# Shifting split weights by 128 and 448 bytes against the activations in a two-layer encoder

## The chip, the cores and the metric

The kernel runs on one core of a Trainium2 chip. The metric is the time of one execution on the device, in microseconds (us).

## The reference

A two-layer encoder over one sequence of 256 tokens of width 1024, all float32. Each layer normalises, multiplies with one wide matrix, runs four mixers side by side (gated linear attention, dilated attention, differential attention, a long convolution), weighs their projections with gates, adds the result, and runs an MLP:

```python
for i in range(DEPTH):                       # DEPTH = 2
    h = rmsnorm(x, norm1_g[i])
    z = h @ w_in[i]                          # 1024 x 11040
    ...
    ya, yb, yc, yd = mixers of the parts of z
    gt = jax.nn.sigmoid(gates.reshape(B, S, N_BRANCH, D_MODEL))
    m = (gt[:, :, 0] * (ya @ proj_a[i]) + gt[:, :, 1] * (yb @ proj_b[i])
         + gt[:, :, 2] * (yc @ proj_c[i]) + gt[:, :, 3] * (yd @ proj_d[i]))
    x = x + m @ w_out[i]
    h2 = rmsnorm(x, norm2_g[i])
    x = x + jnp.square(jax.nn.relu(h2 @ mlp_w1[i])) @ mlp_w2[i]
```

## The kernel before

All large products are done in three matmuls each, with operands split into a rounded upper part and a remainder: upper times upper, upper times lower, lower times upper (`mm3`, L237 to L241, one line for each of the three). The split of activations is kept in tiles `act` (or `h`, `lo`, `u`); the split of weights is made on the way: `load_raw` brings a unit of weights from HBM into one of three slots of the pool `wp` (L206), and `split_to` (L210) makes of each half of it an upper part `hi` on ScalarE (L221) and a lower part `lo` on VectorE (L222), in the pool `hp`, five slots each, some halves ahead of their use.

A matmul here has a stationary operand (`lhsT`), which is loaded into the array by an instruction of its own (PEld in the profile), and a moving one (`rhs`), whose columns run through it. Each matmul has its own load, and the load of the next one runs beside the matmul before. Two ways of use:

- `unit_fm` (L276): the weights are loaded, 128 columns of a part at a time, and the activations move, 256 columns. Units with eight blocks of rows and 256 columns, the gates, `m1` among them, and the `proj` units.
- `chunk_tm` (L243) and the second half of the MLP (`mm` in `mlp`, L1136): the activations are loaded, 128 tokens at a time, and the parts of the weights move, 512 columns (288 in `dv1`). In some units (`stride=2`) the 128 tokens loaded are every second one.

The order of the work is written out by hand: `take` hands out the next half and splits the ones ahead; `tick` (L165) lets the mixers, which are generators, issue a little of their work between units. TensorE's order is thus that of the program.

Places in SBUF follow from the pools in the order of L126 to L132 and from the sizes of their slots: `wp`, `hp` (ten slots of 4096 bytes in each partition), `cp` (constants, among them `r2t` with 32 columns of 4 bytes, of which `inv_ms`, L399, uses two), `s4` (24 slots of 4096 bytes: activations, and tiles of the mixers), `s2` (13 of 2048), `bp`, `sm` (48 small ones). The first slot of `hp` begins at byte 41088 of a partition (128 modulo 512), the first of `s4` at 92352 (192 modulo 512). All slots of `hp`, `s4` and `s2` are multiples of 512 bytes, and the slices that matmuls take begin at multiples of 512 within them, but in `dv1` (rows of 1152 bytes) and where every second token is taken.

Of the kernel before, what the change touches and what calls it, by code (L numbers as in the profile page):

```python
# [10 lines left out]
F32 = mybir.dt.float32  # L11
# [20 lines left out]
def unit_plan():  # L32
    u = {}

    def tm(name, cols):
        for i in range(2):
            u[f"{name}.{i}"] = ("w_in", 4 * i, 4, cols)

    def fm(name, mat, c0, n):
        for i in range(n):  # L40
            u[f"{name}.{i}"] = (mat, 0, 8, [(c0 + 256 * i, c0 + 256 * i + 256)])

    fm("gq", "w_in", AQ, 1)
    fm("gk", "w_in", AK, 1)
    tm("gv", [(AV, AV + 512)])
    tm("gr", [(AR, AR + 512)])
    tm("dq0", [(BQ, BQ + 512)])
    tm("dq1", [(BQ + 512, BQ + 768), (BK, BK + 256)])
    tm("dk1", [(BK + 256, BK + 768)])
    tm("dv0", [(BV, BV + 512)])  # L50
    tm("dv1", [(BV + 512, BV + 768), (ALR, ALR + 32)])
    fm("hx1", "w_in", DU + 512, 2)
    fm("hv", "w_in", DU + 1024, 2)
    fm("hx0", "w_in", DU, 2)
    tm("cq", [(CQ, CQ + 512)])
    tm("ck", [(CK, CK + 512)])
    tm("cv", [(CV, CV + 512)])
    for b, nk in (("a", 4), ("b", 2), ("d", 4), ("c", 4)):
        g = "abcd".index(b)
        fm("gate_" + b, "w_in", GA + g * D, 4)  # L60
        for i in range(2):
            u[f"proj_{b}.{i}"] = ("proj_" + b, 0, nk, [(512 * i, 512 * i + 512)])
    for c in range(2):
        for i in range(2):
            u[f"wo{c}.{i}"] = ("w_out", 4 * i, 4, [(512 * c, 512 * c + 512)])
    for i in range(2):
        u[f"m1b.{i}"] = ("mlp_w1", 4 * i, 4, [(0, 512)])
    for j in range(16):
        if j > 1:
            u[f"m1.{j}"] = ("mlp_w1", 0, 8, [(256 * j, 256 * j + 256)])  # L70
        u[f"m2.{j}"] = ("mlp_w2", 2 * j, 2, [(0, 1024)])
    out, off = {}, 0
    for k, (mat, k0, nk, cols) in u.items():
        n = nk * sum(b - a for a, b in cols)
        out[k] = (mat, k0, nk, cols, off, n)
        off += 128 * n
    return out, off


PLAN, WSIZE = unit_plan()  # L80


def layer_order():
    o = []

    def add(name, n=2):
        o.extend(f"{name}.{i}" for i in range(n))

    add("gr")
    add("dv1")  # L90
    add("gq", 1)
    add("gk", 1)
    add("gv")
    for n in ("hx1", "hv", "hx0", "dq0", "dq1", "dk1", "dv0", "cq", "ck", "cv"):
        add(n)
    for b in "adbc":
        for i in range(2):
            o.extend([f"gate_{b}.{2 * i}", f"gate_{b}.{2 * i + 1}", f"proj_{b}.{i}"])
    add("wo0")
    add("wo1")  # L100
    add("m1b")
    for j in range(16):
        if j + 2 < 16:
            o.append(f"m1.{j + 2}")
        o.append(f"m2.{j}")
    return o


def halves(u):

    mat, k0, nk, cols, off, n = PLAN[u]
    w = n // nk
    if nk == 8 or u.startswith("proj"):
        return [((0, nk), (0, w // 2)), ((0, nk), (w // 2, w))]
    return [((0, nk // 2), (0, w)), ((nk // 2, nk), (0, w))]
# [6 lines left out]
class Kern:  # L122
    def __init__(self, ctx, tc, a):
        self.tc, self.nc, self.a = tc, tc.nc, a
        P = lambda name, bufs, **k: ctx.enter_context(tc.tile_pool(name=name, bufs=bufs, **k))
        self.wp = P("wp", NRAW)  # L126
        self.hp = P("hp", NHL)
        self.cp = P("cp", 1)
        self.s4 = P("s4", NS4)
        self.s2 = P("s2", NS2)  # L130
        self.bp = P("bp", 4)
        self.sm = P("sm", 48)  # L132
        self.pw = P("pw", 4, space=bass.MemoryType.PSUM)
        self.pm = P("pm", 4, space=bass.MemoryType.PSUM)
        self.dp = P("dp", 1, space=bass.MemoryType.DRAM)
        self.n = 0
        self.units = [(l, u) for l in range(L) for u in layer_order()]
        self.halves = [(i, j) for i, (l, u) in enumerate(self.units) for j in range(len(halves(u)))]
        self.ri = self.hi_ = self.ci = 0
        self.raw, self.ready = {}, {}  # L140
        self.evq, self.mixq = [], []
        self.credit = 0.0
# [67 lines left out]
    def split_to(self, upto):  # L210
        nc = self.nc
        while self.hi_ < min(upto, len(self.halves)):
            i, j = self.halves[self.hi_]
            self.load_raw(i + 1)
            hs = halves(self.units[i][1])
            (k0, k1), (c0, c1) = hs[j]
            src = self.raw[i][:, k0:k1, c0:c1]
            if j == len(hs) - 1:
                del self.raw[i]
            hi, lo = [self.hp.tile([128, k1 - k0, c1 - c0], F32, tag=t, name=self.nm(t)) for t in ("hi", "lo")]  # L220
            nc.scalar.copy(hi.bitcast(F32R), src)  # L221
            nc.vector.tensor_sub(lo.bitcast(F32R), src, hi)  # L222
            self.ready[self.hi_] = (hi.bitcast(F32R), lo.bitcast(F32R))
            self.hi_ += 1
            self.load_raw(i + NRAW)
# [173 lines left out]
    def inv_ms(self, tb):  # L399

        nc = self.nc
        s = self.r2t[:, tb:tb + 1]
        nc.vector.tensor_scalar(s, self.ss[tb][:, 0:1], self.ss[tb][:, 1:2], 1.0 / D, ALU.add, ALU.mult)
        nc.vector.tensor_scalar_add(s, s, EPS)
        nc.vector.reciprocal(s, s)
        return s
# [7 lines left out]
    def setup(self):  # L414
        nc, a, cp = self.nc, self.a, self.cp
        self.x = [self.t4([128, D], "x") for _ in range(2)]
        for c in range(2):
            nc.sync.dma_start(self.x[0][:, c * 512:(c + 1) * 512], a["x"][0:128, c * 512:(c + 1) * 512])
        self.ident = cp.tile([128, 128], F32, name="ident")
        nc.sync.dma_start(self.ident, a["ident"])  # L420
        self.gcol = self.ts([128, 8], "gcol")
        nc.sync.dma_start(self.gcol, a["gcol"])
        self.load_raw(1)
        nc.sync.dma_start(self.x[1], a["x"][128:256, :])
        self.load_raw(2)
        self.one = cp.tile([128, 1], F32, name="one")
        nc.vector.memset(self.one, 1.0)
        self.mhalf = cp.tile([128, 8], F32, name="mhalf")
        self.r2t = cp.tile([128, 32], F32, name="r2t")
        nc.vector.memset(self.mhalf, -0.5)  # L430
        self.lrT = cp.tile([33, 256], F32, name="lrT")
        nc.vector.memset(self.lrT[32:33, :], 1.0)
        ones = self.t2([128, 512], "ones")
        nc.vector.memset(ones, 1.0)
        self.load_gain()
        warm = self.ps([128, 512])
        for i in range(3):
            nc.tensor.matmul(warm, lhsT=ones[:, 0:128], rhs=ones, start=True, stop=True)
        self.z0 = cp.tile([33, 256], F32, name="z0")
        nc.sync.dma_start(self.z0, a["z0"])  # L440
        self.gm = cp.tile([128, 4, 256], F32, name="gm")
        graw = self.load_const("gm", [128, 4, 256])
        self.mask = cp.tile([128, 128], I32, name="mask")
        nc.sync.dma_start(self.mask, a["mask"])

        def later():
            yield 0.0
            yield 0.0
            nc.scalar.copy(self.gm.bitcast(F32R), graw)
            yield 0.0  # L450

        self.evq.append(later())
# [763 lines left out]
            self.mlp(act, last)  # L1216


NS4, NS2, NRAW, NHL, LA = 24, 13, 3, 5, 4


@with_exitstack
# [94 lines left out]
```

## Time and profile before

| | us |
|---|---|
| median of 3 runs | 1119.98 (1119.62 to 1120.13) |
| profiled execution, whole | 1119.67 |
| its span, first to last instruction | 1117.9 |
| TensorE busy in the span | 1100.9 (98%) |
| VectorE busy | 729.9 (65%) |
| ScalarE busy | 582.0 (52%) |
| GpSimd busy | 65.5 (6%) |

The page counts an engine as busy while one of its instructions runs; matmuls overlap one another, so that a matmul's duration is longer than the time to the next one's start. The timeline lists instructions by start, and the pace of matmuls is read from there, as the difference of two starts divided by the number of steps between.

### The profile page before, as it was taken

The page shows a single profiled execution, that of the slowest core. Times are in us where ns is not written, and L with a number is a line of the kernel's source. Part 1 is how long each engine was busy: PE and PEld are TensorE (multiplying, and loading weights), DVE is VectorE, ACT ScalarE, POOL GpSimd, SP SyncE. Part 2 cuts the span into 40 slices and gives each one's busy share as a digit, 9 for nine tenths or more (in the row PEclk, how much of TensorE's full clock was granted, in tenths as well). Part 3 has the DMA queues.
Part 4 walks back from the last instruction along what each step waited for, and adds up shares of the span by engine and source line. Part 5 has one row for each costly group of instructions (what it writes and reads, how often), then busy time and mean ns, then how long its engine had stood idle before and what let it go on. Part 6 is the DMA issues. An engine that isn't in the chain of part 4 may idle for free.

```text
span 1117.9 us, 17949 instructions
## 1 busy us (share of the span) xinstructions
PE 1100.9 (98%) x7374; PEld 983.6 (88%) x7374; DVE 729.9 (65%) x1053; ACT 582.0 (52%) x902; POOL 65.5 (6%) x72
## 2 busy tenths in 40 slices
PE   7999999999999999999999999999999999999998
PEld 5889878999999788889878997889999988898987
DVE  5787777657767668655565777776587666555554
ACT  6764554555544564453547555555464456545442
POOL 1001133000100000000000013130001000000000
PEclk9999999999999999999999999999999999999999
DMA  8443544845364555445445444547444655454542
GB/s 309 164 148 120 197 156 153 216 160 189 114 225 153 197 205 185 187 155 222 155 149 209 152 140 182 186 133 212 158 161 136 222 189 188 151 218 159 216 161 76
DMA packets 41527, 195.84 MB, mean 175 GB/s; under 512 B 5025, under 2 KB 16194, under 8 KB 20196
## 3 DMA queue, kind: packets, MB, share of 16 engines
q1 hardware_dynamic: 41444, 194.68, 49.1%
q8 instruction: 58, 0.95, 0.3%
q14 instruction: 25, 0.20, 0.1%
HBM read 193.58 MB, written 1.08 MB: 174 GB/s over the span
## 4 chain that ended last, share of the span: by engine, by line
PE 91%; DVE 4%; POOL 2%; issue 1%; DMA 1%; ACT 1%; SPq 0%; DVEq 0%; ACTq 0%; POOLq 0%
PE w L239 22%; PE w L241 22%; PE w L240 21%; PE acc L241 5%; PE acc L239 5%; PE acc L240 5%; PE tp L308 3%; DVE lo L222 2%; POOL s L301 1%; DMA raw<-in_w 1%; PE p L816 1%; PE p L846 1%; PE p L940 1%; PE p L1020 1%; PE p L905 1%
## 5 line engine op out<-in xcount | busy, mean ns | idle before, releaser
L222 DVE TENSOR_TENSOR lo<-raw,hi 128x1024 fp32r<-128x1024 f32 (+2 forms) x352 | 414.6, 1198 | 140.2 <-ACT hi L221 139.1
L239 PE MATMUL w<-act,hi 128*128 128x256 f32 x1440 | 409.7, 285 | 0.0
L241 PE MATMUL w<-act,lo 128*128 128x256 f32 x1440 | 402.2, 279 | 0.0
L240 PE MATMUL w<-act,hi 128*128 128x256 f32 x1440 | 402.0, 279 | 0.0
L221 ACT CAST hi<-raw 128x1024 fp32r<-128x1024 f32 (+2 forms) x352 | 349.1, 1031 | 31.2 <-ACT hi L221 15.5
L239 PEld LDWEIGHTS w<-act,hi 128*128 128x128 f32 x1440 | 270.4, 188 | 9.1 <-issue 4.1
L240 PEld LDWEIGHTS w<-act,hi 128*128 128x128 f32 x1440 | 270.2, 188 | 2.3 <-issue 0.7
L241 PEld LDWEIGHTS w<-act,lo 128*128 128x128 f32 x1440 | 270.7, 188 | 0.0
L239 PE MATMUL w<-hi,act 128*128 128x512 f32 (+1 forms) x416 | 165.9, 399 | 1.5 <-ACT act L395 1.2
L240 PE MATMUL w<-lo,act 128*128 128x512 f32 (+1 forms) x416 | 161.4, 388 | 1.4 <-DVE lo L222 1.4
L241 PE MATMUL w<-hi,act 128*128 128x512 f32 (+1 forms) x416 | 161.3, 388 | 1.3 <-DVE act L316 1.3
L239 PEld LDWEIGHTS w<-hi,act 128*128 128x128 f32 x416 | 79.4, 191 | 18.4 <-issue 1.7
L241 PEld LDWEIGHTS w<-hi,act 128*128 128x128 f32 x416 | 79.4, 191 | 18.3 <-DVE act L316 2.2
L240 PEld LDWEIGHTS w<-lo,act 128*128 128x128 f32 x416 | 79.5, 191 | 17.7 <-DVE lo L222 2.4
L239 PE MATMUL acc<-hi,u 128*128 128x512 f32 x224 | 88.5, 395 | 0.0
L241 PE MATMUL acc<-hi,u 128*128 128x512 f32 x224 | 88.4, 395 | 0.0
L240 PE MATMUL acc<-lo,u 128*128 128x512 f32 x224 | 88.3, 394 | 0.0
L1101 ACT ACTIVATE u<-w 128x512 f32<-128x512 f32 x28 | 16.7, 598 | 116.3 <-PE w L241 116.3
L1103 DVE TENSOR_TENSOR u<-u 128x512 f32<-128x512 f32 x28 | 19.4, 693 | 87.8 <-ACT u L1101 87.7
L1052 ACT ACTIVATE sg<-w 128x512 f32<-128x512 f32 x32 | 19.1, 597 | 87.9 <-PE w L241 87.9
L301 POOL TENSOR_TENSOR s<-s,mhalf 128x8 f32<-128x8 f32 (+2 forms) x32 | 55.4, 1731 | 2.7
L241 PEld LDWEIGHTS acc<-hi,u 128*128 128x128 f32 x224 | 41.9, 187 | 10.4
(231 smaller groups left out, 978.7 us busy)
## 6 DMA issues: line engine op xcount, KB each, us to landing
raw<-in_w SPq DMA_DIRECT2D x166, 1024.0 KB, 4.9
raw<-in_w SPq DMA_DIRECT2D x8, 512.0 KB, 3.3
raw<-in_w SPq DMA_DIRECT2D x4, 576.0 KB, 3.6
b<-bias SPq DMA_DIRECT2D x32, 64.0 KB, 6.5
b<-bias SPq DMA_DIRECT2D x16, 128.0 KB, 7.6
b<-bias SPq DMA_DIRECT2D x8, 256.0 KB, 5.3
w<-in_hw SPq DMA_DIRECT2D x2, 512.0 KB, 6.3
decay<-in_decay SPq DMA_DIRECT2D x2, 512.0 KB, 7.0
```

Source lines behind the costliest of these rows:

```text
L221: nc.scalar.copy(hi.bitcast(F32R), src)
L222: nc.vector.tensor_sub(lo.bitcast(F32R), src, hi)
L239: mm(out, lhsT=lh, rhs=rh, start=start, stop=False)
L240: mm(out, lhsT=lh, rhs=rl, start=False, stop=False)
L241: mm(out, lhsT=ll, rhs=rh, start=False, stop=stop)
L301: self.nc.gpsimd.tensor_tensor(y, x, self.mhalf[:, 0:n], ALU.pow)
L308: self.nc.tensor.transpose(p[:, i, :], s, self.ident)
L816: nc.tensor.matmul(ps[par][:, c0:c0 + k.stop - k.start], lhsT=st.q[g][r, hp, c], rhs=kk, start=True, stop=True)
L846: nc.tensor.matmul(ps[par * 64:par * 64 + 64, :], lhsT=vs(g, kb, 2 * hp + par), rhs=s["t"][par][:, i], start=(i == 0), stop=(i == 3))
L1052: self.unit_fm(f"gate_{b}.{2 * i + j}", act, lambda _, ps: nc.scalar.activation(sg[:, 2 * j:2 * j + 2], ps, AF.Tanh, scale=0.5))
L1101: nc.scalar.activation(r, ps, AF.Relu)
L1103: nc.vector.tensor_mul(sq, r, r)
```

## The change

Parts of weights get slots of 1152 columns (4608 bytes) in place of 1024, and lie in them from column 0 or, in the units in `MOVING`, from column 112 (448 bytes). `MOVING` are the units whose rows are wider than 256 columns, without the projections: those that move. `r2t` goes away and `inv_ms` takes small tiles from the pool `sm`. To make room, `s4` has 23 slots in place of 24 and `sm` 42 in place of 48.

```diff
+MOVING = {u for u, (mat, k0, nk, cols, off, n) in PLAN.items() if n // nk > 256 and not u.startswith("proj")}
+
+def part_offsets(l, u):
+    return (112, 112) if u in MOVING else (0, 0)
...
-        self.sm = P("sm", 48)
+        self.sm = P("sm", 42)
...
-            hi, lo = [self.hp.tile([128, k1 - k0, c1 - c0], F32, tag=t, name=self.nm(t)) for t in ("hi", "lo")]
+            nk, w = k1 - k0, c1 - c0
+            hi, lo = [self.hp.tile([128, 1152], F32, tag=t, name=self.nm(t))[:, o:o + nk * w].rearrange(
+                "p (k c) -> p k c", k=nk) for t, o in zip(("hi", "lo"), part_offsets(*self.units[i]))]
             nc.scalar.copy(hi.bitcast(F32R), src)
             nc.vector.tensor_sub(lo.bitcast(F32R), src, hi)
...
-        s = self.r2t[:, tb:tb + 1]
+        s = self.ts([128, 1])
...
-        self.r2t = cp.tile([128, 32], F32, name="r2t")
...
-NS4, NS2, NRAW, NHL, LA = 24, 13, 3, 5, 4
+NS4, NS2, NRAW, NHL, LA = 23, 13, 3, 5, 4
```

## Rows read from the trace of the kernel before

**Rows 1.** The page: engines (busy us, share of span, instructions); the chain's shares.

```profile
PE 1100.9 (98%) x7374; PEld 983.6 (88%) x7374; DVE 729.9 (65%) x1053; ACT 582.0 (52%) x902; POOL 65.5 (6%) x72
...
PE 91%; DVE 4%; POOL 2%; issue 1%; DMA 1%; ACT 1%; SPq 0%; DVEq 0%; ACTq 0%; POOLq 0%
```

**Rows 2.** Cores: span and mean granted TensorE clock.

```profile
core 0: 1117.9 us, clock 0.999
```

**Rows 3.** Waits of TensorE: line, waited for: total us, times, longest us.

```profile
PE tp L308 <- DVE u L765: 2.8, 4, 1.0
...
PE w L240 <- DVE lo L222: 1.4, 2, 0.9
```

**Rows 4.** Groups by shape, TensorE: out<-in, shapes, count | busy us, mean ns | idle before.

```profile
L240 PE MATMUL w<-act,hi 128*128 128x256 f32 x1440 | 402.0, 279 | 0.0
...
L240 PE MATMUL w<-lo,act 128*128 128x512 f32 x384 | 151.9, 395 | 1.4 <-DVE lo L222 1.4
...
L240 PE MATMUL acc<-lo,u 128*128 128x512 f32 x224 | 88.3, 394 | 0.0
...
L241 PE MATMUL acc<-hi,lo 128*128 128x512 f32 x32 | 12.6, 395 | 0.0
...
L240 PE MATMUL w<-lo,act 128*128 128x288 f32 x32 | 9.5, 298 | 0.0
...
L240 PE MATMUL p<-ck,cq 64*128 64x256 f32 x32 | 4.6, 279 | 0.0
...
L584 PE MATMUL w<-w3h,u 128*128 128x512 f32 x8 | 3.2, 396 | 0.0
```

**Rows 5.** Timeline, TensorE: start us, duration us, line; first and last of 455 steps.

```profile
302.69 0.28 PE L240 MATMUL w<-act,hi 128*128 128x256 f32 x1
...
356.27 0.28 PE L239 MATMUL w<-act,hi 128*128 128x256 f32 x1
```

**Rows 6.** Timeline, the same shape elsewhere; first and last of 87 steps.

```profile
253.24 0.28 PE L240 MATMUL w<-act,hi 128*128 128x256 f32 x1
...
263.10 0.28 PE L240 MATMUL w<-act,hi 128*128 128x256 f32 x1
```

**Rows 7.** Timeline, 512 columns, end of the MLP; first and last of 55 steps.

```profile
1097.62 0.39 PE L240 MATMUL acc<-lo,u 128*128 128x512 f32 x1
...
1110.45 0.39 PE L241 MATMUL acc<-hi,u 128*128 128x512 f32 x1
```

**Rows 8.** Timeline, 512 columns, every second token loaded; first and last of 30 steps.

```profile
148.37 0.39 PE L240 MATMUL w<-lo,act 128*128 128x512 f32 x1
...
155.26 0.39 PE L240 MATMUL w<-lo,act 128*128 128x512 f32 x1
```

**Rows 9.** Timeline, 288 columns; some of the 15 steps between first and last.

```profile
26.45 0.30 PE L239 MATMUL w<-hi,act 128*128 128x288 f32 x1
26.58 0.29 PE L240 MATMUL w<-lo,act 128*128 128x288 f32 x1
26.71 0.30 PE L241 MATMUL w<-hi,act 128*128 128x288 f32 x1
26.85 0.29 PE L239 MATMUL w<-hi,act 128*128 128x288 f32 x1
...
28.45 0.30 PE L239 MATMUL w<-hi,act 128*128 128x288 f32 x1
```

**Rows 10.** Timeline, passage from m2 to m1: last matmul of 512, first of 256 columns.

```profile
468.55 0.40 PE L241 MATMUL acc<-hi,u 128*128 128x512 f32 x1
468.78 0.28 PE L239 MATMUL w<-act,hi 128*128 128x256 f32 x1
```

**Rows 11.** Groups by shape, weight loads: 128 columns and 64 columns.

```profile
L240 PEld LDWEIGHTS w<-act,hi 128*128 128x128 f32 x1440 | 270.2, 188 | 2.3 <-issue 0.7
...
L846 PEld LDWEIGHTS p<-pt,dv 128*64 128x64 f32 x128 | 6.8, 136 | 1.1
```

**Rows 12.** Groups by shape, all engines: the subtraction that makes a lower part.

```profile
L222 DVE TENSOR_TENSOR lo<-raw,hi 128x1024 fp32r<-128x1024 f32 x336 | 403.4, 1221 | 134.8 <-ACT hi L221 133.8 <-PE w L241 0.2
```

## The prediction

> **What bounds the kernel now.** I read the page's first lines, then the waits of TensorE, then the timeline, because what is asked here is smaller than any row of the page. TensorE is busy for 98% of the span and the chain that ended last is 91% TensorE [rows 1]; its clock is granted to 0.999, so it runs at 2.4 GHz throughout [rows 2]. All its waits for other engines are nine rows that make 12.6 us, the largest 2.8 us in four waits [rows 3]. So the kernel is as long as its matmuls take to follow one another, and other engines matter only through those 12.6 us. What a matmul costs is not its duration in the listing (279 ns for 256 columns [rows 4]), since matmuls overlap; it is the time from one start to the next. Three kinds carry the kernel: 3 x 1440 = 4320 with 256 columns (`unit_fm`), 3 x (384 + 224 + 32) = 1920 with 512 (`chunk_tm` and the second half of the MLP), and 96 with 288 [rows 4].
>
> With 256 columns there are two paces. From 302.69 to 356.27 us lie 455 steps, 117.8 ns each [rows 5]. From 253.24 to 263.10 us the same lines, with the same tiles' places, do 87 steps of 113.3 ns [rows 6]. The timeline has six stretches of the second pace, 24 to 96 matmuls long, 312 in all; the other 4008 or so go at 117.8. With 512 columns the usual step is 233.3 ns (55 steps from 1097.62 to 1110.45 us) [rows 7], and 229.7 where the activations are read every second token (30 steps from 148.37 to 155.26 us) [rows 8]. In sum 4320 x 117.5 + 1920 x 233 + 96 x 133 = 508 + 447 + 13 = 968 us of the 1117.9; the 133 is 15 steps from 26.45 to 28.45 us [rows 9].
>
> The two paces of one line are the main finding. Nothing differs between them in shape, clock or number of bytes; the pace is set at the start of a unit and then stays for 24 to 96 matmuls, through changes of bank and of weights. What can differ is how the loading of the next weights lies in time against the columns of the running matmul: both read SBUF, and each matmul in these rows has its load beside it. So a collision of the two readers is the likely cause, though the trace doesn't show it as a wait. An address is another way to shift one reader against the other, and that is what the change does.
>
> **The change, part by part.** *Addresses.* In the program of before, the first weights' part lies at byte 41088 of a partition and the first tile of the pool s4 at 92352: modulo 512, 128 and 192. Part slots are 4096 bytes and the pools s4 and s2 start alike, so all parts lie 64 bytes below all activations, loaded or moving. The change makes ten part slots 512 bytes larger (no effect modulo 512) and takes `r2t`, 128 bytes, from ahead of s4: activations go to 64, so a part at offset 0 lies 64 above, and a part at offset 448 at the same byte. In the matmuls with 256 columns the load thus goes from 64 below to 64 above what moves. In those with 512 or 288, where the activation is loaded, it goes from 64 above to 0.
>
> *512 columns.* Distance 0 is in the trace already. L584 (512 columns, load and moving both in s4 and s2) has 396 ns against 395 and 394 for the usual rows [rows 4]. At each passage from `m2` to `m1` one matmul moves parts while parts are loaded: 468.55 to 468.78 us is 230 to 240 ns, as beside it [rows 10]. These are few or single matmuls, but with 512 columns a load (188 ns [rows 11]) ends before the next matmul starts, so little is carried on. Ends: all 1824 or so at 233.3 go to 229.7, as in [rows 8]: 1824 x 3.6 = -6.6 us; or all rise by 4 ns, as the 288s differ among themselves (130 to 140 ns by the starts in [rows 9]): +7.7 us. I take 0, by the nearest rows, those at distance 0.
>
> *256 columns.* 64 above with 256 columns is nowhere in the trace. Distance 0 in this shape is L240 of `cq` and `ck`: 279 ns, as the usual 279 [rows 4], on half the rows of the array. The 288s have loads both 64 above and 64 below (their second k lies 128 bytes further), and the steps run from 130 to 140 ns without either side ahead [rows 9]. That speaks against a large effect; the two paces speak for one. Ends: all 4008 go to 113.3 ns, 4008 x 4.45 = -17.8 us; or all rise by the 4 ns just named, +16 us. What an address does here is to set where the pace starts and which of two lasts; now the slow one lasts in 93% of the matmuls, so any shift has more to gain than to lose. I take half of them at the fast pace: -8.9 us. Half is a choice: no row decides it, and both ends stay in the range.
>
> The Trainium skill speaks against this change: "TensorE: Matmul & The Clock Gate", Part 2, step by step, says that TensorE reads SBUF through two independent ports and that loading the next weights takes no bandwidth from the running matmul. By that rule the sum of both kinds would be 0 and the time that of before. Its section on the back-to-back gap gives N/2.4 + 2.5 ns, an estimate of 109 and 216 ns for 256 and 512 columns; the trace has 117.8 and 233.3, so about 9 and 17 ns are left that the page has no cause for.
>
> *The rest.* The casts and subtractions (L221, L222) do the same bytes at another offset, the subtractions 336 times at 1221 ns [rows 12]; VectorE is hidden behind TensorE there, which waited for it 1.4 us in all [rows 3]; if they were slower that wait would grow. I take 0. s4 loses one of 24 slots. In program order at most 20 are between first and last use, so three instead of four are spare; a late slot delays ACT or VectorE, and TensorE waits for them 2.8 us at most in one row [rows 3]: 0 to +2 us, taken as 0. sm goes from 48 to 42 slots and takes the two columns of `inv_ms`; it holds only small columns with few alive: 0. No DMA, wait or queue changes.
>
> Sum: the profiled execution is 1119.67 us (span 1117.9 and 1.8 around it), 0.3 under the median 1119.98. 1119.67 + 0 - 8.9 = 1110.8; on the median 1111.
>
> **The rivals.** (a) *Collision removed throughout.* All 256-column matmuls at 113.3 and the 512s at 229.7: -17.8 - 6.6, so 1095 us; with only the first, 1102. For it: a pace, once taken, lasts for whole units [rows 6]. Against it: the rows at distance 0 show no gain.
> (b) *The distance doesn't matter.* If it counts only within 64 bytes or less, all distances of before and after are alike: 1120 us, give or take 2 for a few units that start in the other pace. For it: rows at distance 0, and both sides in the 288s, all as usual [rows 4, 9]. Against it: nothing but the two paces. The skill's rule on the ports would give this too.
> (c) *Slower.* A load of 64 columns takes 136 ns and one of 128 takes 188 [rows 11], so the load reads at about 0.81 ns a column, while the moving columns take 0.45 (233.3/512) [rows 7]: moving goes at nearly twice the load's speed. Before, the load lies behind the moving columns; after, it lies 64 bytes, 16 columns, ahead of them, and they run into it right at the start and may stay behind it. If each 256-column matmul then loses 2 to 4 ns, that is +9 to +17 us: 1129 to 1137. It decides if the load starts reading together with the moving columns; if it starts over 7 ns (16 x 0.45) later, they have passed the place.
> (d) *It doesn't do what it says*, say if pools were placed otherwise: the addresses follow from sizes alone, so I give it nothing beyond (b).
>
> **How the numbers follow.** Chances: forecast (1111, own range 1103 to 1117) 0.35; rival (a) with all above it 0.20; (b) 0.28; (c) 0.17. A measurement of this kernel can tell 0.2%, 2.2 us, from no change. Faster by more: forecast and (a), 0.55; within: (b), 0.28; slower: (c), 0.17. The range reaches from inside (a), 1095, to 1124, which takes in all of (b) and the mild part of (c); (c) in full and more than (a) are left out, some 0.2.
>
> **What would show it.** Right: in the timeline the steps of 256-column matmuls at about 113 ns in clearly more than six stretches, their mean duration down from 279 towards 276, with the 512s still at 394 to 395. (a) would show the latter at 391 to 392 too. (b) would leave the counts of both paces; (c) would show steps of 120 ns and more. Wrong in another way: new waits of TensorE for ACT or VectorE beyond 12.6 us, which would point to the lost slot of s4; or a third pace, below 113 or above 118, which no row here has and which my sum doesn't price.

## The result, and the profile after

The changed kernel takes 1109.15 us (median of 4 runs, 1108.84 to 1109.56) against 1119.87 us of the kernel before on the same chip: a ratio of 0.9904, 95% interval 0.9887 to 0.9922, so 10.7 us less. The forecast was 1111. The time came out as said; the two terms of the sum did not, as the steps show below.

The page of the changed kernel, engines and the chain's shares (all lines of the code from L222 on lie some nine lines further down):

```profile
PE 1089.1 (98%) x7374; PEld 979.8 (89%) x7374; DVE 729.4 (66%) x1053; ACT 581.8 (53%) x902; POOL 65.3 (6%) x72
...
PE 91%; DVE 4%; POOL 2%; issue 1%; ACT 1%; DMA 0%; SPq 0%; DVEq 0%; POOLq 0%; ACTq 0%
```

What bounds it is what bounded it before [rows 1]: the span is 1107.1 us, TensorE is busy for 98% of it with the same 7374 matmuls and makes 91% of the chain, and the granted clock is 1.000 against 0.999 [rows 2], the level of 2.4 GHz. The waits of TensorE, the two largest and the one for the lower part:

```profile
PE tp L317 <- DVE u L773: 2.5, 4, 1.0
PE p L446 <- DVE ones L442: 2.0, 1, 2.0
...
PE w L249 <- DVE lo L231: 1.4, 2, 1.0
```

In all, nine rows of 13.7 us against 12.6 [rows 3]: the slot that s4 lost and the moved parts cost some 1 us at most. So the gain must lie in the steps from one matmul to the next. The groups by shape (count | busy us, mean ns | idle before):

```profile
L249 PE MATMUL w<-act,hi 128*128 128x256 f32 x1440 | 402.7, 280 | 0.0
...
L249 PE MATMUL w<-lo,act 128*128 128x512 f32 x384 | 150.6, 392 | 1.4 <-DVE lo L231 1.4
...
L249 PE MATMUL acc<-lo,u 128*128 128x512 f32 x224 | 87.4, 390 | 0.0
...
L250 PE MATMUL acc<-hi,lo 128*128 128x512 f32 x32 | 12.4, 389 | 0.0
```

Beside [rows 4], the 512s fell from 394 or 395 to 389 to 392 ns, and the 256s rose from 279 to 280. Durations only hint, since matmuls overlap; the timeline has the pace. The same instructions as in [rows 5 to 8], each by its first and last start (start us, duration us, line), with 455, 87, 55 and 30 steps between:

```profile
300.04 0.28 PE L249 MATMUL w<-act,hi 128*128 128x256 f32 x1
...
353.62 0.28 PE L248 MATMUL w<-act,hi 128*128 128x256 f32 x1
...
250.80 0.28 PE L249 MATMUL w<-act,hi 128*128 128x256 f32 x1
...
261.05 0.28 PE L249 MATMUL w<-act,hi 128*128 128x256 f32 x1
...
1087.33 0.39 PE L249 MATMUL acc<-lo,u 128*128 128x512 f32 x1
...
1099.80 0.39 PE L250 MATMUL acc<-hi,u 128*128 128x512 f32 x1
...
147.49 0.39 PE L249 MATMUL w<-lo,act 128*128 128x512 f32 x1
...
154.49 0.39 PE L249 MATMUL w<-lo,act 128*128 128x512 f32 x1
```

The long stretch of 256s is as slow as before, 53.58/455 = 117.8 ns. The stretch that was fast in [rows 6] is now slow as well, 10.25/87 = 117.8. The 512s at the end of the MLP went from 233.3 to 12.47/55 = 226.7, a pace that no row of before has. The 512s with every second token loaded went the other way, from 229.7 to 7.00/30 = 233.3. And a stretch of 256s that was slow is fast now, 70 steps that took 8.25 us before, 117.8 ns (the first pair of lines), and 7.94 after, 113.4 ns (the second):

```profile
101.48 0.28 PE L240 MATMUL w<-act,hi 128*128 128x256 f32 x1
...
109.73 0.28 PE L241 MATMUL w<-act,lo 128*128 128x256 f32 x1
```

```profile
100.75 0.28 PE L249 MATMUL w<-act,hi 128*128 128x256 f32 x1
...
108.69 0.28 PE L250 MATMUL w<-act,lo 128*128 128x256 f32 x1
```

All steps of the timeline added up by kind (the same ones in both kernels; steps more than 20% over N/2.4 ns, waits among them, left aside):

| steps of the kind | number | mean before, ns | mean after, ns | difference, us |
|---|---|---|---|---|
| 256 columns | 4220 | 117.46 | 116.61 | -3.6 |
| 512, load without gaps | 1477 | 233.29 | 227.82 | -8.1 |
| 512, every second token loaded | 369 | 231.78 | 233.47 | +0.6 |
| everything else | | | | +0.3 |
| sum, before rounding | | | | -10.7 |

The +0.3 is steps of 512 columns that were left aside. The table holds the whole gain, and some 70% of it (-8.1 and +0.6) come from the term that the prediction put at 0.

Below, "distance" is the byte at which the next load starts less the byte at which the running matmul's moving columns start, modulo 512, both from the program's addresses. Before, it was 448 (64 below) for 256 columns and 64 for 512; after, 64 and 0. A "stretch" is a run of at least ten steps of one shape and distance; its pace is the mean step of its second half. With 256 columns there are 101 stretches: 6 fast ones before (306 of 4219 steps at 113.3 ns), 44 after (1252 steps).

### The profile page after: what moved, and what is told of

It is laid out like the page before. It is cut to its first block, busy times and chain, and to the rows that moved or that the text cites. A ratio compares the mean times of both kernels' runs of the same rounds, so it can differ in the third digit from the quotient of the medians.

```text
span 1107.1 us, 17951 instructions
## 1 busy us (share of the span) xinstructions
PE 1089.1 (98%) x7374; PEld 979.8 (89%) x7374; DVE 729.4 (66%) x1053; ACT 581.8 (53%) x902; POOL 65.3 (6%) x72
## 4 chain that ended last, share of the span: by engine, by line
PE 91%; DVE 4%; POOL 2%; issue 1%; ACT 1%; DMA 0%; SPq 0%; DVEq 0%; POOLq 0%; ACTq 0%
PE w L248 22%; PE w L250 22%; PE w L249 22%; PE acc L248 5%; PE acc L249 5%; PE acc L250 5%; PE tp L317 3%; DVE lo L231 2%; POOL s L310 2%; PE p L824 1%; PE p L854 1%; PE p L1028 1%; PE p L948 1%; PE p L913 1%; PE w L614 1%
```

## The experiments

All diffs are against the changed kernel, but where said. The kernel before took 1119.7 to 1120.0 us beside each of them, and the granted clock was 0.996 to 1.000 in the profiled runs that are read here.

**The slots without the distances.** Does anything but the addresses count? Slots, pools and `inv_ms` as changed, `r2t` kept for its room alone, so that all distances are those of before.

```diff
-    return (112, 112) if u in MOVING else (0, 0)
+    return (0, 0)
...
+        self.r2t = cp.tile([128, 32], F32, name="r2t")
+        nc.vector.memset(self.r2t, 0.0)
```

> The slots of the change (4608 bytes for a part, 23 in s4, 42 in sm, inv_ms in sm) with r2t kept as an unused tile and all parts at column 0, so that every part lies 64 bytes below every activation, as in before. Theory D (the distance between what is loaded and what moves sets the pace) and theory P (the byte modulo 512 at which the moving operand itself begins sets it) both expect before's time, 1120 us within 1.5, with 512 columns at 233.3 ns a step and 256 mostly at 117.8. Rival S (something else about the slots brings the gain): 1109 us.

Measured: 1119.98 us, ratio 1.000 (0.9991 to 1.001). The means are 117.46 and 233.29 ns, those of before. Larger part slots, one slot of s4 less and fewer small tiles do nothing; the addresses do it all. Whether it is the places themselves or the distance between them is what the next three runs ask.

**One half of the change alone.** All offsets 0: activations at 64, all parts at 128, so 256 columns have distance 64 as after, and 512 columns 448.

```diff
-    return (112, 112) if u in MOVING else (0, 0)
+    return (0, 0)
```

> The change with all parts at column 0: activations begin at 64 modulo 512, all parts at 128. Moving parts of 512 columns begin at 128 as in before, what is loaded beside them lies 64 below in place of 64 above. 256 columns as in after (part loaded 64 above). Theory P: 512 columns at 233.3 ns, the 256s as after, so some 3.6 us under before, 1116 us. Theory D: only distance 0 is known to be fast, so 64 below gives 233.3 as well or some other pace; a pace of 226.7 here would speak against D in its plain form.

Measured: 1106.80 us, ratio 0.9883 (0.9869 to 0.9898), 2.3 us under the whole change by the medians; the two intervals just overlap, and the steps added up say 1.7. The 512s are worse than after, 229.6 ns on the mean against 227.8, and the 256s better, 115.5 against 116.6, although their own distance is the same 64: 74 of the 101 stretches are fast, against 44. A unit of `m1` in the MLP, here and in the changed kernel, each with the last 512-column matmul ahead of it and its own first and last step:

```profile
476.20 0.39 PE L250 MATMUL acc<-hi,u 128*128 128x512 f32 x1
476.43 0.28 PE L248 MATMUL w<-act,hi 128*128 128x256 f32 x1
...
481.78 0.28 PE L250 MATMUL w<-act,lo 128*128 128x256 f32 x1
```

```profile
475.46 0.39 PE L250 MATMUL acc<-hi,u 128*128 128x512 f32 x1
475.69 0.28 PE L248 MATMUL w<-act,hi 128*128 128x256 f32 x1
...
481.22 0.28 PE L250 MATMUL w<-act,lo 128*128 128x256 f32 x1
```

47 steps take 5.35 us (113.8) here and 5.53 us (117.7) there. What differs is what runs before: the matmuls ahead move parts from byte 128 here and from 64 there. That is taken up again below. The 512s at the end of the MLP, first and last of 55 steps as in [rows 7]:

```profile
1085.51 0.39 PE L249 MATMUL acc<-lo,u 128*128 128x512 f32 x1
...
1098.10 0.40 PE L250 MATMUL acc<-hi,u 128*128 128x512 f32 x1
```

12.59 us, 228.9 ns a step, where the changed kernel has 226.7. The loaded activations lie at byte 64 in both, so the load's own place doesn't set the pace either.

**The other half alone.** `r2t` kept, so activations at 192 and moving parts at 64: 512 columns have distance 128, 256 columns 448 as before.

```diff
+        self.r2t = cp.tile([128, 32], F32, name="r2t")
+        nc.vector.memset(self.r2t, 0.0)
```

> r2t kept, so activations stay at 192 modulo 512; parts that move at column 112, so at 64 modulo 512; the load beside them is 128 above. 256 columns exactly as in before (64 below). Theory P: the moving part begins at 64 as in after, 226.7 ns, about 1478 steps of 6.6 ns less, so 7 to 10 us under before: 1110 to 1113 us. Theory D: distance 128 is not 0, so 233.3 ns and before's time, 1119 to 1121 us.

Measured: 1118.40 us, ratio 0.9986 (0.9977 to 0.9995). The 512s go at 232.3 ns on the mean, not at 226.7 or 227.8, though the moving parts lie at the very byte (64) where the changed kernel has them. So it isn't the moving part's own place; that theory (P) falls. The same 55 steps, 12.78 us, 232.4 ns each:

```profile
1096.71 0.39 PE L249 MATMUL acc<-lo,u 128*128 128x512 f32 x1
...
1109.49 0.39 PE L250 MATMUL acc<-hi,u 128*128 128x512 f32 x1
```

**Distance 0 at another place.** `r2t` with 16 columns, all offsets 0: activations and parts all at byte 128.

```diff
-    return (112, 112) if u in MOVING else (0, 0)
+    return (0, 0)
...
+        self.r2t = cp.tile([128, 16], F32, name="r2t")
+        nc.vector.memset(self.r2t, 0.0)
```

> r2t kept with 16 columns, so activations begin at 128 modulo 512, as do all parts: distance 0 everywhere, but the moving part of 512 columns begins at 128 as in before. Theory D: 226.7 ns with 512 columns, so at least 7 us under before, 1113 us or less, the 256s at distance 0 unknown. Theory P: 233.3 ns with 512 columns; the 256s begin to move at 128 in place of 192 or 64, unknown.

Measured: 1122.93 us, ratio 1.003 (1.0017 to 1.0043), slower than before. Its 512s have the mean of the changed kernel, 227.8, at other bytes and the same distance; the 55 steps of [rows 7] take 12.47 us in both, 226.7 each. Its 256s, now at distance 0 as well, go at 120.0 ns; the stretch of [rows 5], 455 steps in 54.60 us:

```profile
1101.29 0.39 PE L249 MATMUL acc<-lo,u 128*128 128x512 f32 x1
...
1113.76 0.39 PE L250 MATMUL acc<-hi,u 128*128 128x512 f32 x1
...
304.61 0.28 PE L249 MATMUL w<-act,hi 128*128 128x256 f32 x1
...
359.21 0.28 PE L248 MATMUL w<-act,hi 128*128 128x256 f32 x1
```

So the distance sets the pace, not the places, and one distance is the best seen for 512 columns and worse than before for 256.

**Distances in steps of 64 bytes.** The MLP's units at eight offsets, in one kernel.

```diff
+    if u[:3] in ("m1.", "m2."):
+        o = 16 * (int(u[3:]) % 8)
+        return (o, o)
     return (112, 112) if u in MOVING else (0, 0)
```

> The change, but in the MLP the parts of m1.j (loaded) and m2.j (moving) lie at column 16 x (j modulo 8), so each unit has another distance, in steps of 64 bytes: load minus moving is 64 + 64 x (j modulo 8) modulo 512 for m1 (256 columns) and -64 - 64 x (j modulo 8) for m2 (512 columns). Theory D in full (the distance modulo 512 sets the pace): m2.7 and m2.15 (distance 0) at 226.7 ns, m2.0 and m2.8 (64 below) at 229.6, the unit at 64 above (m2.6, m2.14) at 233.3, those at 128 above (m2.5, m2.13) between 230 and 235, the rest new; m1.7 and m1.15 (distance 0) at 120, m1.8 (64 above) at 113.3 or 117.8, m1.6 and m1.14 (64 below) at 117.8. Rival G (only a period of 128 bytes or less counts): units whose distances differ by 128 alike, so m2.7 as m2.5, m2.3, m2.1.

Measured: 1113.3 us (one run). Paces in ns, by distance:

| distance, bytes | 0 | 64 | 128 | 192 | 256 | 320 | 384 | 448 |
|---|---|---|---|---|---|---|---|---|
| 512 columns | 226.7 | 233.3 | 231.7 to 232.8 | 233.3 | 226.7 | 233.3 | 231.7 | 233.3 |
| 256 columns | 120.0 | 113.3 or 117.8 | 118.5 to 120 | 117.8 | 120.0 | 113.3 | 119.1 to 120 | 117.8 |

Each entry has two to six stretches, but for 256 columns at 64 (69) and 512 at 0 (38). Of the 512s at 0, four short stretches, ten or eleven steps each, have 231. The table repeats after 256 bytes, and not after 128. For 256 columns 64 and 320 are the only ones with the fast pace in this kernel; the kernel before, at 448, has it in 6 stretches of 101, so a distance with two or four stretches may have a pace that they don't show.

**Distances in steps of 4 bytes.** `m1.j` at column j, `m2.j` at column 112 + j.

```diff
+    if u[:3] == "m2.":
+        o = 112 + int(u[3:])
+        return (o, o)
+    if u[:3] == "m1.":
+        o = int(u[3:])
+        return (o, o)
     return (112, 112) if u in MOVING else (0, 0)
```

> The change, but in the MLP the parts of m2.j (moving) lie at column 112 + j and those of m1.j (loaded) at column j, so distances go in steps of 4 bytes: load minus moving -4 x j for m2, 64 + 4 x j for m1. Theory L (what counts is which 64-byte line each reader is in): the pace of m2 stays near 226.7 ns for small j and goes over to the 229.6 of 64 below within the 16 steps, at one place. Rival C (the two readers' place counts to the column): it changes with every step or in steps of a few columns.

Measured: 1113.99 us (one run). Paces in ns, two to four stretches each (38 for 512 columns at 0):

| 512 columns at | 0 | 508 | 504 | 500 | 496 | 492 | 488 | 484 | 480 | 476 | 472 | 468 |
|---|---|---|---|---|---|---|---|---|---|---|---|---|
| pace | 226.7 | 237.7 | 232.4 | 229.0 | 231.8 | 236.7 | 233.4 | 227.8 | 233.3 | 234.9 | 234.2 | 230.0 |

| 256 columns at | 72 | 76 | 80 | 84 | 88 | 92 | 96 | 100 | 104 | 108 | 112 | 116 |
|---|---|---|---|---|---|---|---|---|---|---|---|---|
| pace | 118.3 | 113.3 | 118.8 | 120.0 | 113.3 | 118.4 | 118.5 | 120.0 | 117.8 | 122.2 | 119.8 | 118.9 |

The two distances left on each side, 464 and 460, 120 and 124, have 233.3 and 233.3, 119.4 and 120.0. The units at 0 (`m2.0`) and at 508 (`m2.1`) of the second layer, 11 steps each in 2.49 and 2.62 us:

```profile
946.12 0.39 PE L254 MATMUL acc<-hi,h 128*128 128x512 f32 x1
...
948.61 0.39 PE L256 MATMUL acc<-hi,lo 128*128 128x512 f32 x1
...
958.24 0.40 PE L256 MATMUL acc<-hi,lo 128*128 128x512 f32 x1
...
960.86 0.40 PE L255 MATMUL acc<-lo,h 128*128 128x512 f32 x1
```

One column of 4 bytes moves a 512-column step by 11 ns (0 against 508). So neighbours within 64 bytes are not alike: the place counts to the column. For 256 columns the few stretches at 76 and 88 have only the fast pace.

**What chooses between two paces at distance 64.** `m1` stays at distance 64 throughout; only the place of the parts that the matmuls before it move alternates from unit to unit.

```diff
+    if u.startswith("m2."):
+        return (112, 112) if int(u[3:]) % 2 == 0 else (0, 0)
     return (112, 112) if u in MOVING else (0, 0)
```

> The changed kernel with the parts of m2.j at column 0 for odd j and 112 for even j; all m1 parts stay 64 bytes above what moves. What changes for a unit of m1 is only the matmul that stands before its first one. Theory F (at distance 64 the first steps of a unit choose which of two paces lasts): units of m1 behind an m2 of odd j go at 113.3 ns, as in the kernel with all offsets 0, those behind an even j at 117.8, as in the changed kernel: alternating, some 670 steps 4.4 ns faster and 384 of 512 columns 2.5 ns slower, about 1107. Rival G (the pace is set elsewhere, say by what other engines do at the time): no alternation, m1 units as in the changed kernel, 1109 to 1110.

Measured: 1108.96 us (one run). Two units of `m1`, one behind the odd `m2.5` and the next behind the even `m2.6`; again the matmul ahead, the first and the last step:

```profile
464.51 0.40 PE L252 MATMUL acc<-hi,u 128*128 128x512 f32 x1
464.75 0.28 PE L250 MATMUL w<-act,hi 128*128 128x256 f32 x1
...
470.09 0.28 PE L252 MATMUL w<-act,lo 128*128 128x256 f32 x1
...
475.45 0.39 PE L252 MATMUL acc<-hi,u 128*128 128x512 f32 x1
475.67 0.28 PE L250 MATMUL w<-act,hi 128*128 128x256 f32 x1
...
481.21 0.28 PE L252 MATMUL w<-act,lo 128*128 128x256 f32 x1
```

47 steps in 5.34 us (113.6), then 47 in 5.54 us (117.9). The passage itself is 0.24 us before the fast unit and 0.22 before the slow one. Of the 24 stretches of `m1` that stand right behind an `m2`, the 12 behind an odd one are fast and the 12 behind an even one slow, without exception; all 24 are fast with all offsets 0, and all 24 slow in the changed kernel. So at distance 64 what runs ahead of the first step chooses the pace, and it lasts for the unit. The edit moves all 24 matmuls of an `m2` unit; that it is the last of them, which runs beside the unit's first load, is argued. Nor is byte 128 enough: with all offsets 0, the first stretch of `m1` in the first layer stands behind a matmul of `m1b` that moves from 128, and is slow. Its passage took 227 ns. In the three kernels the stretches of `m1` behind an `m1b` or `m2` are slow where the passage took 225 to 227 ns and fast where it took 230 to 236, so the pace goes with the length of that passage. The gain in time (1107 was expected) was eaten by the other side: the `m2` units at distance 448 went mostly at 233.3 ns (12 of 15 stretches, 3 at 229), where the kernel with all offsets 0 has 229 in 60 of 64. That distance has two paces too; what chooses there wasn't tried.

**A distance of 320 for the loaded parts.**

```diff
-    return (112, 112) if u in MOVING else (0, 0)
+    return (112, 112) if u in MOVING else (64, 64)
```

> The changed kernel with the loaded parts at column 64 of their slots instead of 0, so that the load lies 320 bytes above what moves instead of 64; the moving parts stay at distance 0. Theory D (the distance of the two readers modulo 512, to the column, sets the pace): in the sweep 320 gave 113.3 ns in all five units, where 64 gave 113.3 or 117.8; so the 4220 steps of 256 columns go from a mean of 116.6 to 113.3-113.8, -12 to -14 us, and the time is 1095 to 1097; steps of 512 columns stay at 226.7. Rival S (64 and 320 are alike, and the five units were lucky in what stood before them): both paces again, mean 115.5 to 117.8, 1104 to 1114.

Measured: 1109.64 us, ratio 0.9907 (0.9893 to 0.9922): no better than the change, and 13 to 15 us over what the theory had. 43 of 101 stretches are fast, and 100 of the 101 have the pace that they have in the changed kernel. 320 is 64 again: the rival holds. The five fast stretches of the sweep must then have had their pace from what stood before them, which wasn't tried by itself. That distances 256 bytes apart are the same is the firmer for it.

**A distance of 76 for the loaded parts.**

```diff
-    return (112, 112) if u in MOVING else (0, 0)
+    return (112, 112) if u in MOVING else (3, 3)
```

> The changed kernel with the loaded parts at column 3 of their slots, 12 bytes further: the load lies 76 bytes above what moves instead of 64. Theory D: the fine sweep had 113.3 ns at 76 in its units, so 1095 to 1097 as for 320. Rival S (the pace at such distances hangs on how the unit starts): a mix of 113.3 and 117.8 or more, 1104 to 1114. Rival A (a part at a byte that isn't a multiple of 64 costs ScalarE and VectorE, who write it): waits of TensorE for them grow beyond 13.7 us.

Measured: 1096.85 us, ratio 0.9795 (0.9778 to 0.9811), 12.3 us under the changed kernel. 100 of 101 stretches are fast, behind whatever stands before them (the other one has 120.0), and 4220 steps of 113.76 instead of 116.61 ns make 12.0 of the 12.3 us. The page, the group and the stretch of [rows 5], 455 steps in 51.56 us, 113.3 ns:

```profile
PE 1078.2 (98%) x7374; PEld 968.1 (88%) x7374; DVE 729.3 (67%) x1053; ACT 581.5 (53%) x902; POOL 65.2 (6%) x72
...
L249 PE MATMUL w<-act,hi 128*128 128x256 f32 x1440 | 398.1, 276 | 0.0
...
298.45 0.28 PE L249 MATMUL w<-act,hi 128*128 128x256 f32 x1
...
350.01 0.28 PE L248 MATMUL w<-act,hi 128*128 128x256 f32 x1
```

Parts at a byte that isn't a multiple of 64 cost their writers nothing: VectorE and ScalarE are busy as long as in the changed kernel, and TensorE's waits sum to 12.6 us against 13.7.

**Units with every second token loaded.** On top of 320 bytes, the moving parts of these units at column 96, which gives back the distance of before, 64.

```diff
-    return (112, 112) if u in MOVING else (0, 0)
+    if u[:3] in ("dq0", "dq1", "dk1", "dv0"):
+        return (96, 96)
+    return (112, 112) if u in MOVING else (64, 64)
```

> As the kernel with 320 bytes, and in dq0, dq1, dk1 and dv0, where every second token is loaded, the moving parts at column 96 instead of 112, so that this load lies 64 bytes above what moves (the distance of the kernel before) instead of 0. In the changed kernel these 369 steps have a mean of 233.5 ns against 231.8 before. Theory D: 0.5 to 0.7 us less than with 320 alone (up to 1.4 us if all take 229.7). Rival: the form with every second token has the same pace at both distances, no difference.

Measured: 1108.84 us, ratio 0.9901 (0.9886 to 0.9916). The 369 steps fell from a mean of 233.35 to 231.22 ns, 0.8 us, and the median by 0.8 us. The two intervals overlap, so it is the steps that show it.

**The same form at eight distances,** on top of 76 bytes.

```diff
+    two = {"dq0.0": 0, "dq0.1": 16, "dq1.0": 32, "dq1.1": 48, "dk1.0": 64, "dk1.1": 80, "dv0.0": 104, "dv0.1": 93}
+    o = two.get(u, 112 if u in MOVING else 3)
+    return (o, o)
-    return (112, 112) if u in MOVING else (0, 0)
```

> The kernel with 76 bytes, and the eight units with 512 columns that load every second token at eight distances, load minus moving modulo 512: dq0.0 448, dq0.1 384, dq1.0 320, dq1.1 256, dk1.0 192, dk1.1 128, dv0.0 32, dv0.1 76 (the second block of tokens 4 bytes more). This load steps through every second column of 4 bytes. Theory D: the pace goes with the distance here too, but by another table than for loads without gaps, since 0 gives 226.7 ns there and 233.4 here and 64 gives 233.3 there and 231.2 here; some distance among the eight should give 226.7 to 229, others 233 or more. Rival: this form has only 231 to 233.5 at any distance, and the 226.7 needs a load without gaps.

Measured: 1096.5 us (one run). Mean steps in ns, 40 to 46 for each distance and the one 4 bytes above it (second block of tokens):

| distance | 32 | 76 | 128 | 192 | 256 | 320 | 384 | 448 |
|---|---|---|---|---|---|---|---|---|
| mean step | 233.3 | 233.3 | 231.5 | 233.1 | 233.3 | 231.6 | 231.6 | 233.0 |

With 0 (233.5, changed kernel) and 64 (231.2) that is all between 231 and 233.5, and it repeats after 256 bytes too: 231.2 to 231.6 at 64, 320, 128 and 384, 233.0 to 233.5 at the other six. None of the ten gives 226.7: the rival holds as far as they go. Since single columns count with loads without gaps, distances between the ten could still differ.

**Both edits.** 76 bytes, and 96 for the units with every second token.

```diff
-    return (112, 112) if u in MOVING else (0, 0)
+    if u[:3] in ("dq0", "dq1", "dk1", "dv0"):
+        return (96, 96)
+    return (112, 112) if u in MOVING else (3, 3)
```

> The kernel with 76 bytes, with the moving parts of dq0, dq1, dk1 and dv0 at column 96 (their load, of every second token, 64 bytes above what moves). The two edits touch different units, so their gains should add: 1096.85 us less the 0.8 us that the second gave on top of 320 bytes, 1096.0 (0.979 of the kernel before). If they act on each other through the start of a unit (the units behind dv0 and dq take another first pace), it would be 1096.5 to 1097.

Measured: 1096.43 us, ratio 0.9791 (0.9775 to 0.9807), the fastest kernel of this study by its median, 23.6 us under the kernel before. The steps of the units with every second token fell by 0.8 us again; by the times the 0.4 us to the kernel with 76 bytes alone is within the interval.

## Why the prediction was right, and where it wasn't

**What bounds the kernel: right.** The reading of starts instead of durations is what made the change visible at all: after it the duration of the 256s rose from 279 [rows 4] to 280 ns while their step fell by 0.85 ns. TensorE's waits rose by 1.1 us, to 13.7, so nothing else took over.

**The cause: right as far as it can be seen.** "An address is another way to shift one reader against the other": the kernel with the slots alone has the time of before, and one with the same distance elsewhere has the changed kernel's pace with 512 columns, while the same place of the load or of the moving part at another distance has not. How the two reads meet inside isn't in any trace; that they do collide is argued from paces that hang on their distance modulo 256 bytes, to the column. Against it stood the Trainium skill, "TensorE: Matmul & The Clock Gate", Part 2, with two independent ports and a load that takes no bandwidth from the running matmul, which gave no change. The runs don't bear that out: between 226.7 and 237.7 ns for 512 columns, and 113.3 and 122.2 for 256, with nothing changed but addresses.

**The term of the 512s: wrong, 0 taken, -7.5 us measured** (-8.1 and +0.6). The failed step is "Distance 0 is in the trace already". It is there only in other forms. L584, which weighed most, loads every second column, and that form has 231 to 233.5 ns on the mean at ten distances, 0 among them: the row couldn't show what a load without gaps does. The passage from `m2` to `m1` [rows 10] is one step, and a single step says little: it took 0.24 us ahead of a unit that then went fast, and 0.22 ahead of one that went slow. The third witness, `cq` and `ck` with 256 columns, has 64 rows; there two matmuls start 10 ns apart and the next two some 109 ns later, 59.7 ns a step before and after, so that its 279 ns was no pace. That form hid the other sign as well: full 256-column matmuls at distance 0 go at 120 ns. And the remark that little is carried on with 512 columns, since a load of 188 ns ends before the next start, has no support: these steps move by up to 11 ns with one column of distance.

**The range for it: too short on the good side.** Its end, 229.7 [rows 8], came from the stride form as well; 226.7 is below every pace that the rows of before have for 512 columns. The bad ends of both kinds, 4 ns a step, have no row behind them: the 130 and 140 ns of [rows 9] are starts listed to 10 ns, around a mean of 133.

**The term of the 256s: right in mechanism, too large.** -8.9 us was half of all slow steps; 1252 of 4219 are fast after, where half would have made some 2260, and the mean fell by 0.85 ns, -3.6 us. "The pace is set at the start of a unit and then stays" was right, and the step that failed is "half is a choice": at this distance it is decided by what runs before a unit, as the units of `m1` show. In the changed kernel the 24 stretches behind an `m2` that moves from byte 64 are slow; with those parts at byte 128 they are all fast. So the two halves of the change work against each other there: the better distance for the 512s makes the slow start for the 256s, which is why one half alone gave 1106.80. That the sum came out within 2 us is luck: two errors of opposite sign, 7.5 us more gain with 512 columns and 5.3 less with 256.

**The rest: right.** Slots, casts, subtractions and `inv_ms` at 0: 1119.98 us with all of them and the old distances.

**The rivals.** (a) asked for all 256s at 113.3 and 512s at 229.7, 1095 us. The changed kernel showed one half of it, the 512s, and there went below 229.7; the kernel with 76 bytes came to 1096.85. (b) is out by the result and the sweeps. (c) had the mechanism that a load 64 bytes ahead is run into; at 64 no stretch is slower than 117.8, the pace of before, so not there. Slower is possible all the same: at distance 0 the 256s made 1122.93 us. Of the marks that the text gave for its forecast, one held, the fast pace in clearly more than six stretches (44). Two failed in the profile: the 512s, still at 394 to 395 by the text, fell to 389 to 392 ns, and the duration of the 256s, which was to fall towards 276, rose to 280.

## What to carry to other kernels

When a kernel is one long row of matmuls, take the pace from start to start, and look for one shape with two paces: it means that something outside the shape sets it, and here that was where the operands lie, worth 1% in the change and 2% at 76 bytes, without touching the work. A row serves as a witness for a distance only if load and moving operand have the same form as the matmuls it stands for; gaps in the load or half the rows make it another case. Prefer a distance that has one pace whatever stands before it over one that has two, and try the distances inside one kernel, unit by unit, before settling on one; a pace in such a sweep counts only when units with different predecessors show it.

## What the runs showed of the hardware

- The pace depends on the distance of load and moving columns, repeats after 256 bytes (with 256 columns 100 of 101 stretches alike at 64 and 320; with 512 columns 226.7 at 0 and at 256) and changes with single columns of 4 bytes (226.7 at 0, 237.7 at 508).
- The best paces are 113.3 and 226.7 ns: 6.7 and 13.3 ns over N/2.4, one sixteenth in both. So what is left grows with the columns. The Trainium skill, "TensorE: Matmul & The Clock Gate", section "Back-to-back issue gap", has a constant one, N/2.4 + 2.5 ns; no run here shows it.
- Two paces can both last at one distance: with 256 columns at 64 bytes 113.3 or 117.8 ns, chosen by what runs ahead of the first step (24 of 24 stretches behind an `m2`). What chooses at 448, with 512 columns 229 or 233.3, stays open.
- A load of every second token keeps 512-column steps at 231 to 233.5 ns on the mean, at all ten distances that were tried.
